# Route stage of a two-layer decoder trunk: choosing experts from PSUM operands, three tiles at once, and a fixed order into the first expert

## The chip, the cores and the metric

The kernel runs on one core of a Trainium2 chip. The metric is the device time of one execution in microseconds (us), from first to last instruction with what lies around them. Engines are named as the profile names them: PE (TensorE matmuls), PEld (TensorE weight loads), DVE (VectorE), ACT (ScalarE), POOL (GpSimd) and SP (SyncE, which issues most loads).

## The reference

The kernel computes a decoder trunk of two layers on 512 tokens of 1024 columns, in fp32. Layer 0 mixes by sliding-window attention and forgetting attention, layer 1 by sparse top-k attention and latent attention. Each mixer ends in an output projection; then come a layer norm, a mixture of 16 experts (hidden width 512) and a second layer norm:

```
for l in range(2):
    x = layer_norm(ALPHA * x + mixer[l](x), ln_g[l, 0], ln_b[l, 0])
    s = sigmoid(x @ router_w)                 # (512, 16)
    sel = s + router_b                        # 4 groups of 4 experts
    group = argmax over groups of (sum of the best two sel in the group)
    e1, e2 = the two experts of that group with the largest sel
    gate_j = s[e_j] / (s[e_1] + s[e_2])
    y = sum_j gate_j * (silu(x @ w_gate[e_j]) * (x @ w_up[e_j])) @ w_down[e_j]
    x = layer_norm(ALPHA * x + y, ln_g[l, 1], ln_b[l, 1])
```

The router's weights and bias are shared by both layers.

## The kernel before

The 512 tokens are four tiles of 128 rows, `xr[0]` to `xr[3]`. Every large product is made of three passes: a weight chunk of 1 MB is loaded into `wraw`, ScalarE rounds it to a high part (`wh`, L185, 128x1024 at a time), VectorE takes the low part (`wl`, L186), and `mm3` (L198 to L200) adds three matmuls. Activations are split alike by `split_to` (L203 on ScalarE, L204 on VectorE).

The route stage of a layer is `out_proj`. Its pieces run in the order that ROUTE_ORDER (L55) spells out: `y` i adds the second half of the output projection to tile i, in two column halves c (`half_proj`, twelve matmuls each; the sum and its statistics are L571 and L572 on VectorE), transposes the half (L576, TensorE), copies it to `yT` (L578, ScalarE) and multiplies it with the folded router weights into the logits `lgs` (L580, TensorE). `l` i makes mean and inverse deviation, the router's input `u` (L586, L587), the sigmoid `aff` (L588) and the layer norm (L589 on ScalarE, then multiplication by the gain and addition of the bias on GpSimd, L255 and L256; of tile 3 the last 256 columns on VectorE, by LN1_DVE). The normed tile goes to DRAM twice (`x1d`, `yd`, issued on POOL's queue, L591 and L594). `r` i j stands for `choose` (L413 to L454: group and two experts of tiles i to j - 1), `slots` (the place of each token among the tokens of expert 0, L477, and the mask `oh0`, L479) and `first_rows` (L490: the rows of the first expert collected by matmuls with the mask).

All of `choose` works on tiny tiles on VectorE, with operands in SBUF; `lgs` takes 128 of the 512 columns of its PSUM bank.

Then `moe` runs the experts. Each takes at most 96 tokens (CAP). Expert 0's rows come from `first_rows`, split by `put_rows` into `gH` and `gL`; those of the others are gathered from `x1d` by an indirect DMA with `idx`, which `after_slots` makes. `up` makes the gate product (24 mm3 matmuls in two chunks), then the up product; `hidden` transposes, `scatter` does the down product and adds the rows to `yd`. The weights of expert e are loaded by SP in the order in which buffers come free; the first sixteen loads are asked for in the order AHEAD, and `slot_of` gives each its buffer.

A planner puts the instructions of an engine in order by readiness; `tc.issue_after` adds an edge of order between two instructions of one engine, and `keep_in_program_order` fixes the order in which they were written. The order of operations on different engines follows from data and buffers.

Of the kernel before, what the change touches and what calls it, by code (L numbers as in the profile page):

```python
# [41 lines left out]
AHEAD = (2, 3, 4, 0, 1, 5, 6, 8, 9, 10, 12, 13, 7, 14, 11, 15)  # L42


LN1_DVE = (0, 0, 0, 256)
# [9 lines left out]
ROUTE_ORDER = "y0 l0 y1 l1 y2 l2 y3 l3 r02 r23 r34"  # L55
# [12 lines left out]
def trunk_kernel(ctx: ExitStack, tc, x_in, even_w_in, even_b_f, even_sinks, odd_w_in,  # L68
# [92 lines left out]
    hold = [None]  # L161
    in_order = [False]
# [25 lines left out]

    def ksplit(w, n, eng=V):

        rows = []
        for u in range(w.shape[1] // n):
            h, l = unit(w[:, u * n:(u + 1) * n, :], eng[u] if isinstance(eng, list) else eng)
            rows += [(h[:, j, :], l[:, j, :]) for j in range(n)]
        return rows

    def mm3(o, lh, ll, rh, rl, first, last):
        T.matmul(o, lh, rh, start=first, stop=False)  # L198
        T.matmul(o, lh, rl, start=False, stop=False)  # L199
        T.matmul(o, ll, rh, start=False, stop=last)  # L200

    def split_to(hdst, ldst, src):
        first(A.copy(hdst, src))  # L203
        first(V.tensor_tensor(out=ldst, in0=src, in1=hdst.bitcast(F32), op=ALU.subtract))  # L204

    def rsqrt(var, eps, n, pin=lambda ins: ins):
# [20 lines left out]
        c = square(q, v)  # L227
        pin(V.scalar_tensor_tensor(out=p, in0=c, scalar=-10.0 / 3, in1=c, op0=ALU.add, op1=ALU.mult))
# [184 lines left out]
    def choose(t0, t1):  # L413

        n = t1 - t0
        ts_ = slice(t0, t1)
        sel = sm.tile([128, NT, NE], F32, name="sel", bufs=1)[:, 0:n]
        V.tensor_tensor(out=sel, in0=aff[:, ts_], in1=rb.unsqueeze(1).to_broadcast([128, n, NE]), op=ALU.add)
        sg = sel.rearrange("p t (g j) -> p (t g) j", j=4)
# [12 lines left out]
        if n == 1:  # L432
            V.scalar_tensor_tensor(out=gs, in0=gs, scalar=gm, in1=desc4.unsqueeze(1), op0=ALU.is_equal, op1=ALU.mult)
            V.tensor_reduce(out=gm2, in_=gs, axis=AX.X, op=ALU.max)
            V.scalar_tensor_tensor(out=sg, in0=gs.rearrange("p t g -> p (t g)").unsqueeze(2).to_broadcast([128, 4, 4]),
                                   scalar=gm2, in1=sg, op0=ALU.subtract, op1=ALU.add)
        else:
            V.tensor_tensor(out=gs, in0=gs, in1=gm.unsqueeze(2).to_broadcast([128, n, 4]), op=ALU.is_equal)
            V.tensor_tensor(out=gs, in0=gs, in1=desc4.unsqueeze(1).to_broadcast([128, n, 4]), op=ALU.mult)
            V.tensor_reduce(out=gm2, in_=gs, axis=AX.X, op=ALU.max)  # L440
            V.tensor_tensor(out=gs, in0=gs, in1=gm2.unsqueeze(2).to_broadcast([128, n, 4]), op=ALU.subtract)
            V.tensor_tensor(out=sg, in0=gs.rearrange("p t g -> p (t g)").unsqueeze(2).to_broadcast([128, 4 * n, 4]),
                            in1=sg, op=ALU.add)
# [6 lines left out]
        f8 = sm.tile([128, NT, 2], F32, name="rf8")[:, 0:n]  # L450
# [3 lines left out]
        V.tensor_tensor(out=M[:, ts_], in0=O[:, ts_, 0, :], in1=O[:, ts_, 1, :], op=ALU.add)  # L454
# [12 lines left out]
    def slots(sl, oh0, t0, t1):  # L467
# [5 lines left out]
        for j in range(1, t1):  # L473
# [19 lines left out]
    def after_slots(sl, oht, flag):  # L493
# [913 lines left out]
```

## Time and profile before

| | |
|---|---|
| median of 3 runs | 1180.2 us (1179.53 to 1184.04) |
| the profiled execution | 1180.26 us |
| its span (first to last instruction) | 1178.5 us |
| mean granted TensorE clock | 0.954 |
| PE, DVE, ACT, POOL busy | 93%, 79%, 65%, 23% of the span |

A time of the trace counts from the start of the span. The shares are means over stages with different limits: attention in the first 240 us and from 540 to 820 us or so, the route stage of layer 0 around 225 to 272 us and of layer 1 around 810 to 860 us, and the experts behind each. A granted clock of 1 stands for 2.4 GHz; the lower of the two levels is 1.2 GHz.

### The profile page before, as it was taken

How to read it: one execution, taken by the hardware profiler on the slowest of the kernel's cores; microseconds unless marked ns; L12 is line 12 of the kernel's file. 1: busy time of each engine (PE TensorE's matmuls, PEld its weight loads, DVE VectorE, ACT ScalarE, POOL GpSimd, SP SyncE). 2: the span in 40 equal slices, each digit the busy share in tenths (PEclk: the TensorE clock that was granted, in tenths of full speed). 3: DMA queues.
4: the chain of work that ended last, by engine and by line, in shares of the span. 5: the costliest groups of instructions: out<-in, count | busy, mean ns of one | idle time of the engine just before them, and what ended most of it. 6: DMA issues, size and time to landing. Idle time of an engine off the chain costs nothing. (4 is left out here: it accounts for less than half of the span.)

```text
span 1178.5 us, 16701 instructions
## 1 busy us (share of the span) xinstructions
PE 1093.0 (93%) x5775; PEld 817.5 (69%) x5775; DVE 934.3 (79%) x1866; ACT 762.3 (65%) x1229; POOL 266.5 (23%) x223
## 2 busy tenths in 40 slices
PE   8999989979999999998599898999799999999982
PEld 7786767867777777776377665777677777777761
DVE  4646756597999999987766998766879999999976
ACT  4556646235888888887435744654268888888862
POOL 2001340251111141112613133003411111411023
PEclk9999999988999999999699998999789999999997
DMA  8314332779999997998512211335699999989972
GB/s 209 117 40 90 75 88 105 255 276 303 302 358 357 350 334 237 361 357 279 183 28 72 73 37 37 107 108 209 240 299 285 365 342 353 339 255 366 371 234 108
DMA packets 139613, 262.25 MB, mean 223 GB/s; under 512 B 11831, under 2 KB 28247, under 8 KB 139520
## 3 DMA queue, kind: packets, MB, share of 16 engines
q1 hardware_dynamic: 129232, 234.62, 57.9%
q0 software_dynamic: 10288, 26.48, 9.1%
q8 instruction: 47, 0.77, 0.3%
q14 instruction: 46, 0.38, 0.1%
HBM read 246.73 MB, written 22.30 MB: 228 GB/s over the span
## 5 line engine op out<-in xcount | busy, mean ns | idle before, releaser
L186 DVE TENSOR_TENSOR wl<-wraw,wh 128x1024 fp32r<-128x1024 f32 (+1 forms) x418 | 503.6, 1231 | 83.3 <-ACT wh L185 74.9
L185 ACT CAST wh<-wraw 128x1024 fp32r<-128x1024 f32 (+3 forms) x436 | 445.7, 1039 | 155.0 <-PE ps_s L200 63.8
L198 PE MATMUL ps_s<-wh,m 128*96 128x512 f32 (+1 forms) x528 | 208.3, 394 | 1.7 <-ACT m L203 1.7
L199 PE MATMUL ps_s<-wl,m 128*96 128x512 f32 (+1 forms) x528 | 206.4, 391 | 0.0
L200 PE MATMUL ps_s<-wh,m 128*96 128x512 f32 (+1 forms) x528 | 205.0, 388 | 0.4 <-DVE m L204 0.4
L200 PEld LDWEIGHTS ps_s<-wh,m 128*96 128x96 f32 x528 | 86.4, 164 | 35.7 <-DVE m L204 1.3
L198 PEld LDWEIGHTS ps_s<-wh,m 128*96 128x96 f32 x528 | 86.7, 164 | 34.8 <-ACT m L203 2.1
L199 PEld LDWEIGHTS ps_s<-wl,m 128*96 128x96 f32 x528 | 86.4, 164 | 31.9 <-issue 0.2
L198 PE MATMUL ps_a<-wh,hH 128*96 128x512 f32 x256 | 102.7, 401 | 3.8 <-ACT hH L203 3.8
L199 PE MATMUL ps_a<-wl,hH 128*96 128x512 f32 x256 | 101.8, 398 | 4.0 <-POOL wl L186 4.0
L200 PE MATMUL ps_a<-wh,hL 128*96 128x512 f32 x256 | 101.0, 394 | 1.3 <-DVE hL L204 1.3
L198 PE MATMUL ps_a<-wh,XH 128*128 128x512 f32 (+2 forms) x224 | 89.4, 399 | 4.3 <-ACT wh L185 3.2
L1100 POOL DMA_INDIRECT m<-x1d,idx x30 | 33.1, 1104 | 255.8 <-PE ps_t L1111 224.2
L200 PE MATMUL ps_a<-wh,XL 128*128 128x512 f32 (+2 forms) x224 | 88.7, 396 | 1.9 <-DVE XL L204 1.9
L1175 POOL DMA_INDIRECT yd<-m,idx x30 | 49.2, 1640 | 177.0 <-ACT m L1174 173.3
L199 PE MATMUL ps_a<-wl,XH 128*128 128x512 f32 (+2 forms) x224 | 88.8, 396 | 0.0
L199 PE MATMUL ps_a<-XL,wh 128*128 128x512 f32 x160 | 65.0, 406 | 0.0
L200 PE MATMUL ps_a<-XH,wl 128*128 128x512 f32 x160 | 64.7, 405 | 0.3 <-DVE wl L186 0.3
L198 PE MATMUL ps_a<-XH,wh 128*128 128x512 f32 x160 | 64.6, 403 | 0.0
L357 ACT ACTIVATE p<-p,nm 128x256 f32<-128x256 f32 (+3 forms) x96 | 50.6, 529 | 17.8 <-DVE nm L350 8.8
L376 ACT COPY pT<-ps_t 128x512 f32<-128x512 f32 (+2 forms) x88 | 43.4, 517 | 28.8 <-PE ps_t L373 28.0
L199 PEld LDWEIGHTS ps_a<-wl,hH 128*96 128x96 f32 x256 | 41.3, 161 | 20.5 <-POOL wl L186 5.4
(327 smaller groups left out, 1918.3 us busy)
## 6 DMA issues: line engine op xcount, KB each, us to landing
wraw<-in_moe_w_up_dram SPq DMA_DIRECT2D x64, 1024.0 KB
wraw<-in_moe_w_gate_dram SPq DMA_DIRECT2D x64, 1024.0 KB
wraw<-in_moe_w_down_dram SPq DMA_DIRECT2D x64, 1024.0 KB
wraw<-in_w_o_dram SPq DMA_DIRECT2D x6, 1024.0 KB
wraw<-in_even_w_in_dram SPq DMA_DIRECT2D x4, 1024.0 KB
x1d<-xr POOLq DMA_DIRECT2D x8, 512.0 KB
yd<-xr POOLq DMA_DIRECT2D x8, 512.0 KB
xr<-yd SPq DMA_DIRECT2D x8, 512.0 KB
```

Of the source, the lines that this page charges most:

```text
L185: first(A.copy(hv, w))
L186: first(eng.tensor_tensor(out=lv, in0=w, in1=hv.bitcast(F32), op=ALU.subtract))
L198: T.matmul(o, lh, rh, start=first, stop=False)
L199: T.matmul(o, lh, rl, start=False, stop=False)
L200: T.matmul(o, ll, rh, start=False, stop=last)
L357: A.activation(out=pt[h], in_=(pt if bias else Sp)[h], func=AF.Exp, bias=nm[:, h:h + 1], scale=(slopes[0][h] if slopes else 1.0), accum_ou ...
L376: A.copy(d_, s_)
L1100: G.indirect_dma_start(out=xg_of[e], out_offset=None, in_=x1d[:, :], in_offset=bass.IndirectOffsetOnAxis(ap=idx[:CAP, e:e + 1], axis=0), b ...
L1175: G.indirect_dma_start(out=yd[:, :], out_offset=bass.IndirectOffsetOnAxis(ap=idx[:CAP, e:e + 1], axis=0), in_=yos[e % 2], in_offset=None, ...
```

## The change

- ROUTE_ORDER becomes `y0 l0 y1 l1 y2 l2 c03 y3 s03 l3 r03`: `choose` runs once for tiles 0 to 2 and once for tile 3, and `slots` and `first_rows` of tiles 0 to 2 are pieces of their own.
- `choose` takes at most one operand from SBUF in each operation; the other lies in PSUM, in scratch columns of the bank that holds `lgs`. The sigmoid is written twice (PSUM and SBUF), the first sum too. The mask `M` becomes a reduction, `oh0` is made tile by tile, and the inverse deviation of one tile uses operations with one tensor operand.
- The statistics of tiles 0 and 1 come from accumulating instructions (`tensor_tensor_reduce` on VectorE, a square on ScalarE). Tile 3's layer norm is made on VectorE by halves (`centre`, `whole`); GpSimd's affine remains for tiles 0 to 2.
- `half_proj` of a tile's second column half holds its last nine matmuls behind the first half's logits (`behind`).
- Everything behind tile 3's `u` has a written order on VectorE: centre 0, choose, centre 1, slots, whole 0, low part 0, whole 1, put 0, low part 1, put 1, low part 2, then inside the first gate product `slot_tokens` and low part 3. The first expert's high parts come on ScalarE behind the sigmoid.
- `after_slots` is split in three: `slot_tokens` (the index, now in fp32), `slot_weights` (behind expert 0's up product) and `for_the_end` (transposed masks and overflow count, at expert 4).
- AHEAD moves load 7 (the second chunk of expert 0's up weights) to the end, and its buffer and that of two work tiles are exchanged. `hH` and `hL` become one tile. The router's folding is queued behind layer 0's last sum of the first half projection.

The core of the diff:

```diff
-AHEAD = (2, 3, 4, 0, 1, 5, 6, 8, 9, 10, 12, 13, 7, 14, 11, 15)
-LN1_DVE = (0, 0, 0, 256)
+AHEAD = (2, 3, 4, 0, 1, 5, 6, 8, 9, 10, 12, 13, 14, 11, 15, 7)
-ROUTE_ORDER = "y0 l0 y1 l1 y2 l2 y3 l3 r02 r23 r34"
+ROUTE_ORDER = "y0 l0 y1 l1 y2 l2 c03 y3 s03 l3 r03"
...
+    def high(w):
+        h, l = (hl.tile([128, 1024], F32R, name="w" + t.lower(), tag=t).rearrange("p (a b) -> p a b", a=2) for t in "HL")
+        return h, l, A.copy(h, w)
+    def low(w, h, l):
+        return V.tensor_tensor(out=l, in0=w, in1=h.bitcast(F32), op=ALU.subtract)
...
+    def scratch(p):
+        return (p[:, 0:64].rearrange("p (t e) -> p t e", e=NE), p[:, 64:128].rearrange("p (t e) -> p t e", e=NE),
+                p[:, 128:144].rearrange("p (t g) -> p t g", g=4), p[:, 144:152].rearrange("p (t c) -> p t c", c=2))
...
-    def choose(t0, t1):
+    def choose(t0, t1, sc):
+        affp, selp, gp, f8 = (t[:, ts_] for t in sc)
-        V.tensor_tensor(out=sel, in0=aff[:, ts_], in1=rb.unsqueeze(1).to_broadcast([128, n, NE]), op=ALU.add)
+        for t in (selp, sel):
+            V.tensor_tensor(out=t, in0=affp, in1=rb.unsqueeze(1).to_broadcast([128, n, NE]), op=ALU.add)
-        V.tensor_tensor(out=pr[:, :, 0:2], in0=sg[:, :, 0:2], in1=sg[:, :, 2:4], op=ALU.add)
+        V.tensor_tensor(out=pr[:, :, 0:2], in0=sg[:, :, 0:2], in1=sp[:, :, 2:4], op=ALU.add)
...
-        V.tensor_tensor(out=M[:, ts_], in0=O[:, ts_, 0, :], in1=O[:, ts_, 1, :], op=ALU.add)
+            return V.tensor_reduce(out=M[:, ts_], in_=O[:, ts_].rearrange("p t c e -> p t e c"), axis=AX.X, op=ALU.add)
...
-        return V.tensor_tensor(out=oh0[:, t0:t1], in0=slot1.unsqueeze(1).to_broadcast([128, n, CAP]),
-                               in1=sl[:, t0:t1, 0:1].to_broadcast([128, n, CAP]), op=ALU.is_equal)
+        for i in range(t0, t1):
+            oh = V.tensor_scalar(oh0[:, i, :], slot1, sl[:, i, 0:1], None, op0=ALU.is_equal)
...
+    def slot_tokens(sl, room):
+        for h in range(2):
+            oh = room()[:, 0:4 * CAP].rearrange("p (j s) -> p j s", j=4)
+            V.tensor_tensor(out=oh, in0=slot1.unsqueeze(1).to_broadcast([128, 4, CAP]),
+                            in1=pos[:, 4 * h:4 * h + 4].unsqueeze(2).to_broadcast([128, 4, CAP]), op=ALU.is_equal)
...
-    def half_proj(chunk, oH, oL, g, i):
+    def half_proj(chunk, oH, oL, g, i, behind=None):
+            with tc.issue_after(behind.ins) if behind and k else nullcontext():
+                mm3(o, oH[4 * g + k][:, ts_], oL[4 * g + k][:, ts_], *chunk[k], k == 0, k == 3)
...
-            lgs = ps_s()[:, 0:2 * NT * NE].rearrange("p (c t e) -> p c t e", c=2, t=NT)
+            bank = ps_s()
+            lgs = bank[:, 0:2 * NT * NE].rearrange("p (c t e) -> p c t e", c=2, t=NT)
+            sc = scratch(bank[:, 2 * NT * NE:512])
...
+                if by_act(i):
+                    V.tensor_tensor_reduce(out=ys, in0=o, in1=ys, scale=1.0, scalar=(ls[:, i, 0:1] if c else 0.0),
+                                           op0=ALU.add, op1=ALU.add, accum_out=ls[:, i, c:c + 1])
...
+                A.activation(out=sc[0][:, i, :], in_=u[:, i, :], func=AF.Sigmoid)
+                end["act"] = A.activation(out=aff[:, i, :], in_=u[:, i, :], func=AF.Sigmoid)
...
+        def centre(h):
+            return V.scalar_tensor_tensor(out=ys, in0=ys, scalar=end["mu"], in1=gb[:, cs], op0=ALU.subtract, op1=ALU.mult)
+        def whole(h):
+            return V.scalar_tensor_tensor(out=ys, in0=ys, scalar=end["rs"], in1=bb[:, cs], op0=ALU.mult, op1=ALU.add)
...
+        with tc.issue_after(end["u"].ins):
+            c0 = centre(0)
+        with tc.issue_after(c0.ins):
+            chosen = choose(n, NT, sc)
+        with tc.issue_after(chosen.ins):
+            c1 = centre(1)
+        with tc.issue_after(c1.ins):
+            oh = slots(sl, oh0, n, NT)
...
-                t = xo.tile([128, 2048], F32, name="wraw3", tag=dict(e=eH, E=eL, l=lL, x=lH)[t])
+                t = xo.tile([128, 2048], F32, name="wraw3", tag=dict(e=eH, E=eL, l=eL, x=lH)[t])
...
+        in_turn(lambda: route["whole"](0))
+        route["rows"](0)
+        low_part(0)
+        in_turn(lambda: route["whole"](1))
+        route["rows"](1)
+        route["x1"]()
+        in_turn(lambda: put_rows(0, ps2[0]))
+        low_part(1)
+        in_turn(lambda: put_rows(1, ps2[1]))
+        low_part(2)
+        def between():
+            with tc.issue_after(last_mm[0].ins):
+                in_turn(lambda: found.extend(slot_tokens(sl, route["room"])) or found[0])
+            low_part(3)
+            for i in (1, 2):
+                gather(i)
...
+            if e == 4:
+                with tc.issue_after(act_op[0].ins):
+                    for_the_end(sl, oht, flag)
```

## Rows read from the trace of the kernel before

**Rows 1.** The page's first part: busy time, share of the span, instructions of each engine.

```profile
PE 1093.0 (93%) x5775; PEld 817.5 (69%) x5775; DVE 934.3 (79%) x1866; ACT 762.3 (65%) x1229; POOL 266.5 (23%) x223
```

**Rows 2.** Windows: length, busy time (instructions) PE, PEld, DVE, ACT, POOL; clock, DMA share, GB/s.

```profile
240.00:250.00 10.00, 7.42 (x25) 6.27 (x26) 8.10 (x35) 3.82 (x5) 3.00 (x3) 0.66 0.59 231
...
300.00:440.00 140.00, 140.00 (x667) 99.54 (x666) 130.27 (x128) 119.61 (x144) 30.35 (x20) 1.00 1.02 343
...
830.00:840.00 10.00, 10.00 (x44) 8.07 (x44) 5.60 (x12) 5.47 (x7) 3.83 (x2) 0.65 0.08 18
```

**Rows 3.** Timeline of PE, both layers: start, duration, operation, count, [idle before <-releaser].

```profile
236.47 1.03 PE L580 MATMUL ps_s<-rwgb,yT 128*128 128x16 f32 x8
...
238.13 0.39 PE L200 MATMUL ps_a<-wh,XL 128*128 128x512 f32 x1
238.36 0.39 PE L198 MATMUL ps_a<-wh,XH 128*128 128x512 f32 x1
...
242.58 0.66 PE L576 MATMUL ps_t<-ident,xr 128*128 128x128 f32 x4 [2.90 <-DVE xr L571]
...
247.27 0.63 PE L200 MATMUL ps_a<-wh,XL 128*128 128x512 f32 x1
247.70 0.63 PE L198 MATMUL ps_a<-wh,XH 128*128 128x512 f32 x1
...
279.52 0.40 PE L200 MATMUL ps_s<-wh,m 128*96 128x512 f32 x1
...
287.65 0.47 PE L198 MATMUL ps_s<-wh,m 128*96 128x512 f32 x1 [0.85 <-ACT m L203]
...
823.24 0.40 PE L200 MATMUL ps_a<-wh,XL 128*128 128x512 f32 x1
...
874.85 0.48 PE L198 MATMUL ps_s<-wh,m 128*96 128x512 f32 x1 [0.85 <-ACT m L203]
```

**Rows 4.** Timeline of DVE and POOL in layer 0's route stage.

```profile
229.19 2.37 POOL L256 TENSOR_TENSOR xr<-xr,lnt 128x1024 f32<-128x1024 f32 x1
229.21 0.69 DVE L571 TENSOR_TENSOR xr<-xr,ps_a 128x512 f32<-128x512 f32 x1 [1.79 <-PE ps_a L200]
...
237.41 2.46 POOL L256 TENSOR_TENSOR xr<-xr,lnt 128x1024 f32<-128x1024 f32 x1
...
237.51 2.40 DVE L423 TENSOR_TENSOR pr<-sel 128x16 f32<-128x16 f32 x1
...
241.85 0.67 DVE L571 TENSOR_TENSOR xr<-xr,ps_a 128x512 f32<-128x512 f32 x1
```

**Rows 5.** Timeline of layer 1's tail, DVE, PE and ACT.

```profile
845.40 0.23 DVE L587 SCALAR_TENSOR_TENSOR u<-ps_s,rs_o,u 128x16 f32<-128x16 f32 x1
...
850.88 0.16 DVE L418 TENSOR_TENSOR sel<-aff,rb 128x16 f32<-128x16 f32 x1
...
853.51 0.17 DVE L454 TENSOR_TENSOR M<-O 128x16 f16<-128x16 f16 x1
...
855.15 0.17 DVE L477 SCALAR_TENSOR_TENSOR sl<-ps_s,M 128x16 f32<-128x16 f32 x1 [1.27 <-PE ps_t L517]
...
855.76 1.99 PE L490 MATMUL ps_o<-oh,xr 128*128 128x96 f32 x8 [0.62 <-DVE oh L479]
...
857.83 0.48 ACT L203 CAST m<-ps_o 128x384 fp32r<-128x384 f32 x1 [11.04 <-issue]
```

**Rows 6.** Groups by line: operation, count | busy, mean ns | idle before it, releasers.

```profile
L186 DVE TENSOR_TENSOR wl<-wraw,wh 128x1024 fp32r<-128x1024 f32 (+1 forms) x418 | 503.6, 1231 | 83.3 <-ACT wh L185 74.9
...
L204 DVE TENSOR_TENSOR m<-ps_t,m 128x384 fp32r<-128x384 f32 x60 | 30.6, 551 | 0.0
...
L578 ACT COPY yT<-ps_t 128x512 f32<-128x512 f32 x16 | 9.3, 586 | 33.3 <-PE ps_t L576 33.3
```

**Rows 7.** Timeline of layer 0's mixer: two engines reading one PSUM tile.

```profile
82.30 0.42 ACT L709 COPY vt<-ps_a 128x316 f32<-128x316 f32 x1 [3.13 <-PE ps_a L200]
...
82.76 0.17 DVE L710 TENSOR_TENSOR z<-ps_a,bf 128x8 f32<-128x8 f32 x1 [3.38 <-ACT vt L709]
```

More of the change, by code (lines that the diff above doesn't have):

```diff
@@ L161, in trunk_kernel @@
     hold = [None]
+    late = [None]
     in_order = [False]
@@ L199, in mm3 @@
         T.matmul(o, lh, rl, start=False, stop=False)
-        T.matmul(o, ll, rh, start=False, stop=last)
+        last_mm[0] = T.matmul(o, ll, rh, start=False, stop=last)
     def split_to(hdst, ldst, src):
         first(A.copy(hdst, src))
-        first(V.tensor_tensor(out=ldst, in0=src, in1=hdst.bitcast(F32), op=ALU.subtract))
+        return first(V.tensor_tensor(out=ldst, in0=src, in1=hdst.bitcast(F32), op=ALU.subtract))
     def rsqrt(var, eps, n, pin=lambda ins: ins):
@@ L566, in out_proj, with room, by_act @@
         rows = [ksplit(wload(chunk_src(c, g), 4, 512), 2) for c in range(2)]
+        def room():
+            return work.tile([128, 512], F32, name="yT", tag="sg", bufs=2)
+        def by_act(i):
+            return main and i < 2
+        sts = [sm.tile([128, 2, 6], F32, name="st", tag="st", bufs=4) for _ in range(NT)]
         def tile_y(i):
@@ new lines, in tile_ln @@
+                A.activation(out=sc[0][:, i, :], in_=u[:, i, :], func=AF.Sigmoid)
+                end["act"] = A.activation(out=aff[:, i, :], in_=u[:, i, :], func=AF.Sigmoid)
+            if i == NT - 1 or not main:
+                end.update(mu=mv[:, 0, 0:1], rs=rs)
+                return
+            nm = sm.tile([128, 1], F32, name="nmr", bufs=4)
+            if by_act(i):
+                V.tensor_scalar(nm, ls[:, i, 2:3], 32.0, rs, op0=ALU.mult, op1=ALU.mult)
+            else:
+                V.tensor_scalar(nm, mv[:, 0, 0:1], -1.0, rs, op0=ALU.mult, op1=ALU.mult)
@@ L591, in tile_ln, with x1 @@
+            with tc.issue_after(end["act"].ins):
+                A.activation(out=xr[i], in_=xr[i], func=AF.Identity, scale=rs, bias=nm)
+            affine(xr[i], gb, bb, 0)
+            x1(i)
+        def x1(i):
             nc.gpsimd.dma_start(x1d[i * 128:(i + 1) * 128, :], xr[i])
@@ L607, in out_proj, with last_rows @@
                 tile_ln(i)
-            else:
-                j = int(n[1])
-                if i == 0:
-                    ps2 = [ps_o(), ps_s()]
-                choose(i, j)
-                slots(sl, oh0, i, j)
-                first_rows(ps2, oh0, i, j)
-        return sl, ps2, oht
+            elif f == "c":
+                choose(i, int(n[1]), sc)
+            elif f == "s":
+                slots(sl, oh0, i, int(n[1]))
+            else:
+                for c, k in enumerate(("y", "lg")):
+                    with tc.issue_after(end[k].ins):
+                        first_rows(ps2, oh0, i, int(n[1]), (c,))
+        n = NT - 1
+        with tc.issue_after(end["u"].ins):
[6 more added lines that the diff above has]
+            oh = slots(sl, oh0, n, NT)
+        def last_rows(h):
+            first_rows(ps2, oh0, n, NT, (h,))
+        return sl, ps2, oht, dict(oh=oh, act=end["act"], whole=whole, rows=last_rows, x1=lambda: x1(n), room=room)
     def even_mixer():
@@ L1204, in moe @@
             sg = act(g, u, n)
+            if e == 0:
+                with tc.issue_after(put.ins):
+                    slot_weights(found[1])
             if e < last:
@@ L1297, in dense_moe @@
             A.activation(out=aff, in_=lgs, func=AF.Sigmoid)
-            choose(0, NT)
+            sc = scratch(ps_o())
+            V.tensor_copy(sc[0], aff)
+            choose(0, NT, sc)
             weights()
```

166 lines of the change are left out of this document (98 added, 68 removed).

## Prediction

> **What bounds the kernel now.** I read the page's busy shares first: TensorE is busy 93% of the span [rows 1], so only a stretch in which it idles or runs slowly can give much back. The windows say where that is. In the expert loop TensorE is busy 140.00 of 140 us at clock 1.00, with the DMA share at 1.02 [rows 2]: nothing on VectorE or ScalarE is to be won there. The windows on the route stage show the opposite: the granted clock is 0.66 in 240 to 250 us and 0.65 in 830 to 840 us, a mix of the two levels, 2.4 and 1.2 GHz [rows 2].
>
> TensorE's timeline gives the reason. The second half projection of tile 2 (call its end E) ends at 238.5 us in layer 0 and 823.6 in layer 1. Soon after, TensorE stands 2.90 us, released by VectorE's residual sum of that half. Behind the stall, matmuls follow each other every 0.43 us (247.27 to 247.70), before it every 0.23 [rows 3]. So a stall of about 3 us was followed by some 7 us at the lower level; the same place of layer 1 has the 0.65 [rows 2].
>
> Who makes VectorE late? The sum at 241.85 is queued behind `choose` of tiles 0 and 1, and of that one addition of 16 numbers a row takes 2.40 us (237.51), exactly while GpSimd runs its 2.4 us multiplications of layer norm (237.41). The sum of 229.21 has one operand in PSUM and ran beside a GpSimd instruction of the same kind in its usual 0.69 us [rows 4]. Two SBUF operands wait for GpSimd; one does not.
>
> The tail repeats it. In layer 1 tile 3's `u` is ready at 845.63, but VectorE then does its quarter of the layer norm beside GpSimd, so `choose` of tile 3 starts only at 850.88 and ends at 853.68 (2.80 us); the slots follow at 855.15, the row products run at half pace (1.99 us for eight), and the second expert's first matmul comes at 874.85 [rows 3, 5].
>
> **The change, part by part.** I count from E to expert 1's first matmul; behind that, TensorE sets the pace. Before, that is 287.65 - 238.52 = 49.1 us in layer 0 and 874.85 - 823.64 = 51.2 in layer 1 [rows 3].
>
> *One SBUF operand each.* The contended additions fall to some 0.2 us. Some 14 operations of the three-tile `choose` and 11 of the one-tile one now touch PSUM. Does that cost more? `sl`, which reads PSUM, takes 0.17 us; an addition in SBUF beside nothing took 0.16 [rows 5]. Lower bound 0; upper bound 0.07 each (`u` reads PSUM in 0.23) [rows 5], 25 x 2 x 0.07 = 3.5 us. I take 0.
>
> *Tile 3 without turns between engines.* Without the stall TensorE runs tile 3's first half at once: 12 x 0.23 = 2.8. The sum 0.69, transposes some 0.7, copy 0.59, logits 1.03 [rows 3, 4, 6] bring it to E+6.0. The nine matmuls held behind these logits end at E+8.2 and cost about 0.3 us against running them early, as TensorE has nothing else. Sum, transposes, copy, logits again 3.0, hand-overs of about 0.1 each, `u` 0.46: E+12.75. Sigmoid some 0.35; VectorE centres the first half beside it (0.69). `choose` measured 2.80 and grows by a doubled first sum and a reduction for the mask, 3.2 in all: E+16.7. Then second centring 0.7 (E+17.4), slots 0.45, one half of the affine 0.69 (E+18.55). The eight row products at full pace take 0.9, the copy 0.48 [rows 5], hand-overs 0.7: first expert matmul E+20.7.
>
> *The fixed order on VectorE.* The first expert's four low parts, 1.23 each [rows 6], were done during tile 3 before; now they are queued in the tail. From E+18.55: low 1.23, whole 0.69, put 0.55, low 1.23, put 0.55, low 1.23, `slot_tokens` 3.2, low 1.23 [rows 6]. (The 3.2 is an estimate: two masks of 384 columns at 0.55, as the low part of that size [rows 6]; three operations on 128 columns, between the 0.16 of 32 and that 0.55, at 0.3 [rows 5]; the matmuls and the index 1.2.) That is 28.6; six last matmuls 1.4 and hand-overs: gate ends at E+30.5. VectorE, not TensorE, sets this. In layer 0 the second expert follows the end of the first gate by 7.7 us (279.92 to 287.65) [rows 3]; with 0.3 for the moved load, 8.0 gives E+38.5. Gains 10.6 and 12.7: 23.3 us.
>
> *Turns on one PSUM bank.* The new scratch columns lie in the bank of the router's logits. Three-tile `choose` (25 operations at about 0.19, from about E+4.3, since it needs tile 2's sigmoid) works in it until E+9, and tile 3's first logits write into the same bank at E+5.1. The trace has one case of two engines at different columns of one bank: VectorE's `z` (columns 316 to 324) starts at 82.76, only after ScalarE's copy of columns 0 to 316 (82.30, 0.42 long), with 3.38 us idle put down to it [rows 7]. I take it that the logits wait as `z` did: they start at E+9.0, 3.9 late, and by the `behind` edge nine projection matmuls wait too. At full clock, less the 0.9 us that VectorE would have made the second half late anyway, 3.0 us a layer. But 3.9 us is longer than the 2.90 that was followed by the lower level. At 0.43 instead of 0.23, nine matmuls cost 1.8 more, and logits, transposes and the second logits another 1.4: 6.2 a layer. Gains 4.4 and 6.5, 10.9 together.
>
> The Trainium skill, "PSUM — Partial Sum Buffer", section "PSUM bank collisions raise a hardware error", speaks against this change: it says that two engines on one bank and partition quadrant must not meet even at different columns, and that the compiler's scheduler therefore adds a dependency between them. The trace agrees in its one case (`z` at 82.76). By it the stall is certain; without it the sum would be the 23.3 above.
>
> *Smaller parts.* Tiles 0 and 1 take the variance on ScalarE (a square of 1024 columns, about 1.2) instead of two VectorE statistics of 0.69; both lie under TensorE's projections: 0, at most 0.5 a layer if it delays a copy to `yT`. Second sigmoid write 0.2, in the sum. GpSimd loses its tile-3 affine; `x1d` and `yd` of tile 3 are issued after the second `whole`, far ahead of the gathers: 0. The count of overflowing tokens and the transposed masks move to expert 4, some 0.3 of TensorE a layer either way: 0. Loads: u1c1 is asked for last and waits for the first gate; it is needed 5 us later, so it may cost 0 to 1. The queue is kept full through the loop [rows 2]: if loads did not come earlier with the issues, a gain would be eaten later; but issues on SP follow buffers that TensorE frees, so I take 0. Sum of small gains 1.
>
> Sum against the profiled execution, 1180.26 us (span 1178.5, 1.8 around it; the median 1180.2 is 0.06 away): 1180.3 - 10.9 - 1 = **1168**.
>
> **The rivals.**
> (a) The logits wait, but the clock stays at 2.4 GHz: 3.0 a layer, 1180.3 - 17.3 = 1163. For it: TensorE has run at 1.00 without a break up to E, and one stall is thin; against it, both layers show the lower level at this place [rows 2].
> (b) No waiting for the bank: 1180.3 - 23.3 = 1157. For it: one example is thin, and the order of the two could be exchanged, logits first. Against: the example.
> (c) Loads eat it: the DMA share is 1.02 in the loop; if half of 12 comes back as waits of ScalarE on loads, 1174.
> (d) No change: `choose` at 25 operations, handed over to and from TensorE, or queued behind VectorE's other work, ends 5.5 us later than I have it, which both layers pay: 1168 + 11 = 1179.
> (e) Slower: an operand in PSUM is dear for a chain of short dependent operations. With 50 on the path, +0.22 us each eats the 11; from +0.34 each the kernel is over 0.5% slower (1186). `sl`'s 0.17 speaks against it [rows 5], but that one has no PSUM operation right ahead of it, as these have.
>
> **How the numbers follow.** Chances: forecast 0.44, (a) 0.18, (b) 0.16, (c) 0.06, (d) 0.08, (e) 0.08. 0.5% is 5.9 us, about what a measurement here can tell from no change. Faster are the first four, less a little of (c): 0.82; same 0.10; slower 0.08. Low end: (b) less 3 for small gains, 1154. High end: the forecast with 3.5 for PSUM and 5 from (c), 1177. (d), (e) and a tail below 1154 are left out, 0.2 together.
>
> **What would show it.** Right: no VectorE addition above 0.3 us beside GpSimd in `choose`; TensorE idle 3 to 4 us near E+5 to E+9, released by an operation of the three-tile `choose`; matmuls every 0.43 us behind it; `choose` of tile 3 right after `u`; the first expert at about E+27, the second at E+45. Wrong for (b) if there is no such wait; for (a) if 0.23 goes on; for (c) if ScalarE waits on loads in the loop; for (e) if the PSUM operations are 0.3 us or their pitch 0.4. The forecast fails most if `choose` is moved on VectorE against tile 3's sums, or if `slot_tokens` takes far from 3.2 us.

## The result and the profile after

The changed kernel takes 1196.6 us (median of four runs, 1193.91 to 1201.05) against 1182.02 for the kernel before in the same comparison: a ratio of 1.0128, 95% interval 1.0085 to 1.0171. The forecast was 1168; the kernel is slower, and by a mechanism that none of the rivals names. The profiled execution took 1193.91 us (span 1192.1), 13.65 more than the one before. One of the nine runs of e5 below, at a granted clock of 0.644 (1586.87 us), is left out of its ratio.

The page's busy line, which answers to [rows 1], differs little:

```profile
PE 1094.6 (92%) x5787; PEld 815.0 (68%) x5787; DVE 922.4 (77%) x1818; ACT 765.9 (64%) x1243; POOL 262.6 (22%) x219
```

The windows [rows 2] do. The columns are those of before: length, busy time of PE, PEld, DVE, ACT, POOL, granted clock, DMA share, GB/s.

```profile
250.00:260.00 10.00, 7.47 (x28) 5.69 (x29) 4.01 (x22) 0.43 (x1) 5.30 (x4) 0.55 0.42 147
...
280.00:300.00 20.00, 17.20 (x71) 12.48 (x71) 13.20 (x19) 10.48 (x13) 5.57 (x3) 0.76 1.01 336
310.00:450.00 140.00, 140.00 (x672) 99.64 (x671) 129.75 (x130) 119.16 (x143) 29.74 (x19) 1.00 1.01 343
```

Ten us of the route stage have a clock of 0.55, and 280 to 300 us, in which the first two experts run, 0.76. In the loop TensorE is busy throughout, as before.

VectorE and GpSimd in layer 0's route stage and first expert (answers to [rows 4] and [rows 5]; start, duration, engine, line):

```profile
249.49 2.33 POOL L272 TENSOR_TENSOR xr<-xr,lnt 128x1024 f32<-128x1024 f32 x1 [1.80 <-ACT xr L662]
...
250.37 0.20 DVE L467 TENSOR_TENSOR sel<-gs,ps_s 128x48 f32<-128x48 f32 x1
...
251.61 0.26 DVE L476 TENSOR_TENSOR O<-io,ps_s 128x96 f16<-128x96 f32 x1
...
257.93 0.69 DVE L624 TENSOR_TENSOR xr<-xr,ps_a 128x512 f32<-128x512 f32 x1 [5.78 <-PE ps_a L210]
...
262.92 0.17 DVE L443 TENSOR_TENSOR ps_s<-ps_s,rb 128x16 f32<-128x16 f32 x1
...
265.67 0.19 DVE L479 TENSOR_REDUCE M<-O 128x16 f16<-128x32 f16 x1
...
277.98 0.17 DVE L537 TENSOR_SCALAR idx<-ps_s 96x16 uint32<-96x16 f32 x1 [1.73 <-PE ps_s L535]
...
279.03 4.61 POOL L1204 DMA_INDIRECT m<-x1d,idx  x1 [8.23 <-DVE idx L537]
279.20 4.85 DVE L186 TENSOR_TENSOR wl<-wraw,wh 128x1024 fp32r<-128x1024 f32 x4
...
283.97 0.30 DVE L484 TENSOR_TENSOR gt<-O,aff 128x128 f32<-128x128 f16 x1
...
287.10 0.16 DVE L488 TENSOR_TENSOR as__2920<-a 128x4 f32<-128x4 f32 x1
287.35 1.23 DVE L186 TENSOR_TENSOR wl<-wraw,wh 128x1024 fp32r<-128x1024 f32 x1
288.49 0.17 DVE L489 RECIPROCAL as__2920<-as__2920 128x4 f32<-128x4 f32 x1
...
290.08 0.29 DVE L542 TENSOR_TENSOR og<-O,gates 128x128 f32<-128x128 f16 x1
```

`choose` does what the change says: 0.15 to 0.3 us an operation even beside GpSimd's multiplication (249.49), 2.94 us for tile 3 (262.92 to 265.86). Further down, the index comes 8.6 us behind the first expert's first matmul (269.40), the gather takes GpSimd 4.61 us beside four low parts in a row, and the small steps from `gt` to `og` wait behind low parts of 1.23 us.

TensorE, same stretch, and two rows of layer 1 (answers to [rows 3]):

```profile
245.95 1.06 PE L633 MATMUL ps_s<-rwgb,yT 128*128 128x16 f32 x8 [0.29 <-ACT yT L631]
...
252.01 1.86 PE L633 MATMUL ps_s<-rwgb,yT 128*128 128x16 f32 x8 [4.99 <-DVE O L476]
...
254.70 0.63 PE L210 MATMUL ps_a<-wh,XL 128*128 128x512 f32 x1
255.13 0.63 PE L208 MATMUL ps_a<-wh,XH 128*128 128x512 f32 x1
...
269.40 0.74 PE L208 MATMUL ps_s<-wh,m 128*96 128x512 f32 x1 [0.57 <-ACT m L213]
...
279.34 0.62 PE L209 MATMUL ps_s<-wl,m 128*96 128x512 f32 x1 [1.39 <-DVE wl L195]
...
290.43 2.74 PE L546 MATMUL ps_t<-og,yT 128*96 128x16 f32 x16 [2.80 <-DVE og L542]
293.00 1.52 PE L1215 MATMUL ps_t<-ident,m 96*128 96x96 f32 x8
294.45 0.74 PE L208 MATMUL ps_s<-wh,m 128*96 128x512 f32 x1
...
848.01 1.86 PE L633 MATMUL ps_s<-rwgb,yT 128*128 128x16 f32 x8 [4.99 <-DVE O L476]
...
887.08 1.52 PE L1215 MATMUL ps_t<-ident,m 96*128 96x96 f32 x8
```

The logits of tile 3's first half stand 4.99 us in both layers until VectorE's last scratch operation of the three-tile `choose` (L476), the pitch behind (from one matmul's start to the next) is 0.43 us (254.70 to 255.13), and the rows of expert 1 are transposed (L1215) only at 293.00 and 887.08. Before, that was 285.97 (L1111).

To compare kernels I cut the profiled executions at marks that all have. A is VectorE's last sum of the first half projection (215.38 us in layer 0 before, 217.28 after). The other marks are the last residual sum, the first expert's first matmul, and the transposes of expert 1's and of expert 2's rows. Each cell is layer 0 / layer 1, in us, differences of starts in the timelines of one execution, so its sums need not follow the medians to the microsecond. The labels are those of the experiments below.

| kernel | A to last sum | to first matmul | to expert 1's rows | to expert 2's rows |
|---|---|---|---|---|
| before | 36.8 / 59.5 | 20.4 / 21.0 | 13.4 / 13.5 | 13.7 / 13.6 |
| after | 40.7 / 64.0 | 11.5 / 11.4 | 23.6 / 22.1 | 14.0 / 13.9 |
| e5_index_early | 40.7 / 64.3 | 12.5 / 15.7 | 19.7 / 19.5 | 15.3 / 14.8 |
| e6_own_bank2 | 36.6 / 58.2 | 14.6 / 15.6 | 23.7 / 20.7 | 14.1 / 14.1 |
| e8_both_no_behind | 31.6 / 53.0 | 16.5 / 15.6 | 18.4 / 19.0 | 14.6 / 14.2 |
| e9_chain_whole | 31.5 / 52.8 | 18.1 / 16.5 | 14.7 / 15.4 | 13.1 / 12.8 |
| b1_operands_only | 35.1 / 56.4 | 17.5 / 16.7 | 15.1 / 14.2 | 15.8 / 13.1 |
| e12_no_behind_alone | 30.8 / 51.7 | 17.6 / 17.9 | 23.7 / 22.1 | 14.2 / 13.9 |

From A to the first matmul the change gains 5.1 and 5.2 us. In the next column it loses 10.2 and 8.6. That, and not the route stage, is where it became slower than before.

### The profile page after: what moved, and what is told of

It reads as the page before. It is cut to its first block, busy times and chain, and to the rows that moved or that the text cites. A ratio compares the mean times of both kernels' runs of the same rounds, so it can differ in the third digit from the quotient of the medians.

```text
span 1192.1 us, 16678 instructions
## 1 busy us (share of the span) xinstructions
PE 1094.6 (92%) x5787; PEld 815.0 (68%) x5787; DVE 922.4 (77%) x1818; ACT 765.9 (64%) x1243; POOL 262.6 (22%) x219
## 4 chain that ended last, share of the span: by engine, by line
PE 37%; DVE 9%; ACT 2%; POOL 1%; issue 1%; DVEq 0%; POOLq 0%; ACTq 0%
PE ps_s L208 5%; PE ps_s L210 5%; PE ps_s L209 5%; PE ps_a L208 5%; PE ps_a L210 5%; PE ps_a L209 5%; DVE sc L1080 1%; PE ps_o L397 1%; PE ps_t L390 1%; DVE m L1079 1%; PE ps_s L1105 1%; PE ps_t L1215 1%; DVE nm L369 1%; DVE mx L364 1%; PE ps_s L633 1%
## 5 line engine op out<-in xcount | busy, mean ns | idle before, releaser
L186 DVE TENSOR_TENSOR wl<-wraw,wh 128x1024 fp32r<-128x1024 f32 (+1 forms) x410 | 494.6, 1233 | 83.5 <-ACT wh L185 74.8
L185 ACT CAST wh<-wraw 128x1024 fp32r<-128x1024 f32 (+3 forms) x428 | 437.3, 1038 | 154.9 <-PE ps_s L210 71.9
L209 PE MATMUL ps_s<-wl,m 128*96 128x512 f32 (+1 forms) x528 | 206.6, 391 | 2.8 <-DVE wl L195 2.8
L209 PEld LDWEIGHTS ps_s<-wl,m 128*96 128x96 f32 x528 | 87.2, 165 | 37.1 <-DVE wl L195 3.2
L209 PE MATMUL ps_a<-wl,h 128*96 128x512 f32 x256 | 101.3, 396 | 5.8 <-POOL wl L186 5.8
L208 PE MATMUL ps_a<-wh,h 128*96 128x512 f32 x256 | 102.8, 402 | 3.7 <-ACT h L213 3.7
L210 PE MATMUL ps_a<-wh,h 128*96 128x512 f32 x256 | 101.7, 397 | 1.3 <-DVE h L214 1.3
L1204 POOL DMA_INDIRECT m<-x1d,idx x30 | 37.4, 1247 | 253.9 <-PE ps_t L1215 236.9
L209 PE MATMUL ps_a<-wl,XH 128*128 128x512 f32 (+2 forms) x224 | 87.1, 389 | 0.0
L209 PE MATMUL ps_a<-XL,wh 128*128 128x512 f32 x160 | 64.6, 404 | 0.0
L209 PEld LDWEIGHTS ps_a<-wl,h 128*96 128x96 f32 x256 | 41.6, 163 | 22.9 <-POOL wl L186 7.1
```

The costliest lines, as they stand in the source:

```text
L185: first(A.copy(hv, w))
L186: first(eng.tensor_tensor(out=lv, in0=w, in1=hv.bitcast(F32), op=ALU.subtract))
L210: last_mm[0] = T.matmul(o, ll, rh, start=False, stop=last)
L1204: G.indirect_dma_start(out=xg_of[e], out_offset=None, in_=x1d[:, :], in_offset=bass.IndirectOffsetOnAxis(ap=idx[:CAP, e:e + 1], axis=0), b ...
```

## The experiments

Each ratio is against the kernel before on the same chip, whose median there was 1178.97 to 1180.86 us (1182.02 beside the changed kernel). Where two kernels were measured beside different runs of the kernel before, their ratios are compared and not their medians. The first four runs took the visible waits: the shared bank, and what delays expert 1.

**e1_own_bank.** The scratch of `choose` goes to free columns of the bank that collects the first rows.

```diff
-            sc = scratch(bank[:, 2 * NT * NE:512])
+            ps2 = [ps_o(), ps_s()]
+            sc = scratch(ps2[0][:, 4 * CAP:512])
```

> The changed kernel, but the scratch of choose lies in the free columns of the bank that collects the first expert's rows, not in the bank of the logits. Theory (turns on one bank): tile 3's logits no longer stand 4.99 us behind the three-tile choose, the matmuls behind them keep 0.23 us instead of 0.43; the last residual sum comes 5 to 6 us earlier in each layer (252 instead of 257.93 in layer 0), the first expert's first matmul too, and the time falls by 9 to 12 us to about 1186. Rival (the chain of short VectorE operations on PSUM operands sets the tail, whichever bank they are in): the stall goes, the first expert's first matmul moves by under 2 us, time 1193 or more.

1198.84 us, ratio 1.0158 (1.0134 to 1.0181). The wait on L476 is gone, but it turned up elsewhere. On VectorE:

```profile
267.05 0.18 DVE L443 TENSOR_TENSOR ps_o<-ps_o,rb 128x16 f32<-128x16 f32 x1 [6.57 <-PE ps_o L516]
```

`choose` of tile 3 now waits 6.57 us for the row products, which write other columns of that bank. So in these two kernels a bank went from engine to engine as a whole, in the written order, and the next try gave the scratch a bank that almost nobody else writes.

**e2_weights_later.** The gate weights (`slot_weights`, the chain from `gt` to `og`) move from behind expert 0's up product into expert 1's gate product.

```diff
-            if e == 0:
-                with tc.issue_after(put.ins):
-                    slot_weights(found[1])
+        def weigh():
+            with tc.issue_after(last_mm[0].ins):
+                slot_weights(found[1])
...
+            g = up("g", e, *((None, 1, weigh if e == 1 else None) if e else (g0, 1, between)))
```

> The changed kernel, but slot_weights stands on TensorE's queue inside expert 1's gate product instead of ahead of expert 1's transposes. Theory (TensorE's queue): the 2.80 us wait for og, its 2.74 us of matmuls and the half pace of the transposes (1.52 instead of 0.82) go from the path; expert 1's transposes start at 288 instead of 293.0 in layer 0 and at 882 instead of 887.1 in layer 1, time 9 to 11 us lower, about 1187. Rival (expert 1's rows are late anyway, since the index comes at 278 and the first gather takes 4.61 us on GpSimd's queue): the transposes wait for the gathered rows, under 1.5 us a layer is won, time 1194 or more.

1196.99 us, 1.0171 (1.0128 to 1.0214): nothing won. TensorE's waits from 240 to 305 us (engine, tile and line that waited, what it waited for, us, times, longest) show why:

```profile
PE ps_s L633 <- DVE O L476: 5.0, 1, 5.0
PE ps_t L1215 <- DMA m<-x1d,idx: 3.5, 1, 3.5
```

Without the wait on `og`, the gather itself is late. The transposes started at 288.15, 7.45 us after GpSimd's instruction of 276.09 to 280.70 had ended. Expert 2's rows came 16.7 us behind expert 1's instead of 14.0: the matmuls on `og` (1.45 us) now stand between them; the rest of the difference is not explained.

**e3_low_first.** Low part 3 goes ahead of `slot_tokens`.

```diff
         def between():
+            low_part(3)
             with tc.issue_after(last_mm[0].ins):
                 in_turn(lambda: found.extend(slot_tokens(sl, route["room"])) or found[0])
-            low_part(3)
```

> The changed kernel, but VectorE makes the first gate's last low part before slot_tokens instead of behind it. Theory (the gate stands behind slot_tokens): TensorE's wait of 1.4 us for that low part and the lower clock behind it go; expert 0's products end 3 to 4 us earlier in each layer, but slot_weights still stands ahead of expert 1, so expert 1 starts only 1 to 3 us a layer earlier: time 1191 to 1195. Rival (the index, 1.2 us later, holds expert 1): expert 1's transposes do not move or come later, 1197.

1189.2 us, 1.0083 (1.0025 to 1.0140), below the 1191 to 1195 that I expected, but with an interval that overlaps the changed kernel's. The wait of L209 on `wl` went and one of 1.5 us on the masks of `slot_tokens` came. The gather took 1.41 us here, not 4.61.

**e4_all_three** puts the three edits together.

> All three edits together. Theory (three places where TensorE's queue stands, each followed by a lower clock): expert 1's transposes come 11 to 13 us earlier than in the changed kernel in each layer (about 281 and, 11 more, 863 to 865), time about 1172, below the kernel before. Rival (the three hide behind one another, VectorE's fixed order sets the end): 1182 or more.

1197.9 us, 1.0157 (1.0118 to 1.0195): a miss. The transposes wait 4.7 us for the gather. The edits open the same wait from several sides, and the row collector's bank (e1) costs more than it saves: its first matmul comes 3.6 and 1.9 us later, counted from A. The gather starts 0.9 us behind the index, so the next runs brought that forward.

**e5_index_early.** `slot_tokens` moves ahead of low part 0, the index behind `put_rows` 0; `slot_weights` goes into expert 0's up product.

```diff
-        low_part(0)
         in_turn(lambda: route["whole"](1))
-        route["rows"](1)
         route["x1"]()
+        in_turn(tokens)
+        route["rows"](1)
+        low_part(0)
         in_turn(lambda: put_rows(0, ps2[0]))
+        in_turn(lambda: slot_index(found[0]))
+        for i in (1, 2):
+            gather(i)
         low_part(1)
         in_turn(lambda: put_rows(1, ps2[1]))
         low_part(2)
+        low_part(3)
```

> The changed kernel with another order behind slots on VectorE: whole 0, whole 1, slot_tokens, low part 0, put 0, the index, then low part 1, put 1, low parts 2 and 3; slot_weights stands inside expert 0's up product. Theory (expert 1 waits for its rows: index, then a gather of 1 to 5 us on GpSimd, then some 7.4 us until the rows are there): the index comes about 15 us behind the last residual sum instead of 20, expert 1's transposes come 7 to 9 us earlier in each layer, counted from the last residual sum (35.1 us behind it in layer 0 of the changed kernel, then 26 to 28), and the time falls by 14 to 18 us to about 1180. Rival (the low parts, now later, hold the gate product, so VectorE sets expert 1 whatever the index does): expert 1's transposes within 2 us of where they were, time 1193 or more.

1190.01 us, 1.0087 (1.0062 to 1.0111). The index is written at 270.98, 7.0 us earlier, and the stretch from the first matmul to expert 1's rows falls from 23.6 and 22.1 to 19.7 and 19.5. But `slot_tokens` now stands ahead of the first matmul, which comes 1.1 and 4.5 us later from A; up to expert 1's rows the profiled execution is 2.8 us better in layer 0 and 2.0 worse in layer 1. Two waits remain, and the gather is as long as in the changed kernel:

```profile
PE ps_t L551 <- DVE og L547: 3.0, 1, 3.0
PE ps_t L1221 <- DMA m<-x1d,idx: 2.2, 1, 2.2
```

```profile
267.97 0.53 POOL L673 DMA_DIRECT2D x1d<-xr  x1 [12.94 <-DVE pt L525]
...
276.86 4.98 POOL L1210 DMA_INDIRECT m<-x1d,idx  x1 [7.84 <-ACT wh L185]
```

The gather starts 5.7 us behind the index, and what held it is the write of tile 3's normed rows to `x1d`, which it reads: issued at 267.97, it landed 7.9 us later, at 275.9, and the gather started 0.96 us behind that. In nine places of the runs (both layers of e5, e7 and e8, layer 1 of the changed kernel, e6 and e12) the gather starts 0.95 to 1.04 us behind this landing; in layer 0 of the changed kernel, e6 and e12, where the index comes later than the landing, it starts 0.88 us behind the index. So bringing the index forward uncovered the next thing that the gather needs.

**e6_own_bank2.** The scratch, and the place products of `slots`, get a third bank of their own.

```diff
-            sc = scratch(bank[:, 2 * NT * NE:512])
+            own = ps_s()
+            sc = scratch(own)
...
-        pp = ps_s()
...
-            oh = slots(sl, oh0, n, NT)
+            oh = slots(sl, oh0, n, NT, own[:, 256:320])
```

> The changed kernel with choose's scratch in a PSUM bank of its own (shared only with the counts pp of slots, whose matmuls come between the two chooses). Theory (turns): tile 3's logits wait only for tile 2's u (about 1.4 us) instead of 4.99 us for the three-tile choose, and choose of tile 3 follows its sigmoid at once; the last residual sum comes 3 to 5 us earlier against the eighth sum of the first half, and so does everything behind it: 1187 to 1190. Rival (as in the first try, the wait moves to the tail): last residual sum to first expert matmul grows from 11.5 to over 15 us, time 1196 or more.

1188.92 us, 1.0083 (1.0051 to 1.0115), within the range that I expected, 0.45% (some 5 us) under the changed kernel. The intervals of e5 and of e6 each overlap the changed kernel's; only both together (e7) stand clear of it. The wait of 4.99 us is gone; the logits wait 1.4 us for `u`, which still reads their bank. From A the last sum comes 4.1 and 5.7 us earlier, but the first matmul only 1.0 and 1.5.

**e7_both** is e5 and e6 together, **e8_both_no_behind** is that without the `behind` edge:

```diff
-                o = half_proj(rows[c], oH, oL, g, i, end.get("lg") if main and c else None)
+                o = half_proj(rows[c], oH, oL, g, i, None)
```

> Early index and own bank together. Theory (two separate causes, a stall ahead of the tail and a late index behind it): the gains add, 1168 to 1175, below the kernel before. Rival (they overlap): not below 1180.

> The same without the edge that holds the last nine projection matmuls behind the first half's logits. Theory (a stall of TensorE costs twice, as wait and as lower clock behind it): the nine matmuls fill the remaining wait for tile 2's u, no stall and no matmuls at 0.43 us before the tail, another 2 to 3 us a layer, 1164 to 1170. Rival (the edge keeps the order that the tail needs; without it the first half's logits and the statistics come later): within 1 us of the run before, or slower.

e7 takes 1182.5 us (1.0035, 1.0004 to 1.0066), 0.93% under the changed kernel, against 0.41 and 0.45 for e5 and e6: the two repairs add up, but the time is the rival's (not below 1180), as e5 had won less than I expected. e8 takes 1176.55 us (0.9968, 0.9939 to 0.9997): the edge that I had put at 0.3 us a layer costs 6 here. It still fell short of the 1164 to 1170 that I expected, and its waits name the rest:

```profile
PE ps_t L550 <- DVE og L546: 3.0, 1, 3.0
PE ps_t L1221 <- DMA m<-x1d,idx: 1.4, 1, 1.4
```

**e9_chain_whole** is e8 with the chain from `gt` to `og` written as one piece right behind low part 3, and the low parts of the up weights behind it. **e10_chain_mid** puts it between low part 1 and `put_rows` 1.

```diff
         low_part(3)
+        in_turn(lambda: slot_weights(found[1]))
...
-            u = up("u", e, None, n, None if e else weigh)
+            with nullcontext() if e else tc.issue_after(put.ins):
+                u = up("u", e, None, n, None if e else weigh)
```

> The last kernel (early index, own bank, no edge behind the logits), and the small operations that lead to og now follow one another on VectorE right behind low part 3, with the up weights' low parts behind them. Theory (TensorE's stall for og, 3.0 us and the lower clock behind it, comes from low parts of 1.23 us that stand between the six small operations): the stall goes or is under 0.5 us, expert 1's transposes come 3 to 5 us earlier, time 1167 to 1171. Rival (the up weights' low parts, pushed back by the chain, stop TensorE instead, or the gathered rows do): less than 1.5 us a layer, 1174 to 1177.

> As the run before, but the small operations stand between low part 1 and put 1, so that GpSimd's first gather can run beside them and not beside back-to-back low parts. Theory (the gather takes 4.6 to 5.9 us instead of 1.1 because VectorE runs low parts back to back): the first gather ends within 2.5 us, the gathered rows no longer hold expert 1, time 1164 to 1169. Rival (the gather's length has another cause): it stays over 4 us, and low parts 2 and 3, 1.5 us later, hold the gate: 1172 or more.

e9 takes 1163.75 us, 0.9849 (0.9802 to 0.9896): faster than both kernels, and more than I expected. e10 takes 1168.51 us, 0.9896 (0.9848 to 0.9943); why it is behind e9, though its marks are not, is not explained. In e9's timeline the chain is whole, and the gather short:

```profile
273.66 0.28 DVE L484 TENSOR_TENSOR gt<-O,aff 128x128 f32<-128x128 f16 x1
...
274.50 0.18 DVE L489 RECIPROCAL as__2850<-as__2850 128x4 f32<-128x4 f32 x1
274.71 0.17 DVE L490 TENSOR_TENSOR gates<-a,as__2850 128x8 f32<-128x8 f32 x1
274.91 0.29 DVE L546 TENSOR_TENSOR og<-O,gates 128x128 f32<-128x128 f16 x1
274.99 1.17 POOL L1216 DMA_INDIRECT m<-x1d,idx  x1 [7.22 <-DVE gates L490]
...
283.18 0.82 PE L1227 MATMUL ps_t<-ident,m 96*128 96x96 f32 x8
```

The six steps take 1.54 us (273.66 to 275.20), against 6.4 in the changed kernel (283.97 to 290.37). What the whole chain and what the shorter gather (1.17 us, in e8 5.64) is worth, e9 does not separate. TensorE's largest waits from 240 to 300 us are now 1.2 and 0.9:

```profile
PE ps_o L515 <- DVE xr L692: 1.2, 1, 1.2
PE ps_s L209 <- DVE wl L186: 0.9, 1, 0.9
```

and in the second of these windows the clock is back (the columns as above):

```profile
240.00:260.00 20.00, 17.97 (x99) 15.35 (x98) 14.64 (x77) 8.20 (x15) 12.75 (x10) 0.81 0.94 345
260.00:300.00 40.00, 37.34 (x211) 28.14 (x211) 33.07 (x46) 23.45 (x30) 6.00 (x6) 0.97 0.85 289
```

In the same two windows the granted clock is 0.74 and 0.83 in the changed kernel, 0.83 and 0.87 in the kernel before.

e10 came within its range, but not for its reason. Its gathers are short, yet not beside the small operations, which had ended 3.3 us earlier; they ran inside a row of low parts:

```profile
273.26 8.06 DVE L186 TENSOR_TENSOR wl<-wraw,wh 128x1024 fp32r<-128x1024 f32 x7
273.91 1.52 POOL L1216 DMA_INDIRECT m<-x1d,idx  x1 [8.01 <-DVE wl L195]
275.73 1.85 POOL L1216 DMA_INDIRECT m<-x1d,idx  x1 [0.31 <-issue]
```

**b1_operands_only** goes from the other side: the kernel before, with PSUM operands in `choose` (scratch in a bank of its own) and `choose` of tiles 0 and 1 written ahead of tile 2, as its planner had run it. The smaller edits of `choose`, `slots` and the inverse deviation that go with the operands (the mask as a reduction, `oh0` tile by tile, the second sigmoid) are in it, nothing else of the change.

```diff
-ROUTE_ORDER = "y0 l0 y1 l1 y2 l2 y3 l3 r02 r23 r34"
+ROUTE_ORDER = "y0 l0 y1 l1 r02 y2 l2 r23 y3 l3 r34"
...
-        V.tensor_tensor(out=pr[:, :, 0:2], in0=sg[:, :, 0:2], in1=sg[:, :, 2:4], op=ALU.add)
+        V.tensor_tensor(out=pr[:, :, 0:2], in0=sg[:, :, 0:2], in1=sp[:, :, 2:4], op=ALU.add)
```

> The kernel before with one part of the change alone: choose, slots and the inverse deviation with one SBUF operand each, scratch in a PSUM bank of its own, choose of tiles 0 and 1 written ahead of tile 2 so that it need not wait for later sigmoids; after_slots, the loads, the low parts and the layer norm stay. Theory (the operands part does what it was forecast to do: no addition of 2.4 us, no stall of 2.9 us and no lower clock behind it): last residual sum 4 to 6 us earlier in each layer, choose as fast as before, time 1168 to 1173. Rival (operands in PSUM cost as much as they save, or handing the bank over does): 1178 or more.

1174.34 us, 0.994 (0.9918 to 0.9963). The groups of instructions from 230 to 262 us (busy us, mean ns of one, idle before) show the additions of `choose` cheap; their first ones, from 240.06 us on, ran beside GpSimd's multiplication (238.90 to 241.29):

```profile
L433 DVE TENSOR_TENSOR ps_s<-ps_s,rb 128x32 f32<-128x32 f32 (+1 forms) x2 | 0.4, 182 | 0.1
...
L437 DVE TENSOR_TENSOR pr<-sel,ps_s 128x16 f32<-128x16 f32 (+1 forms) x2 | 0.3, 160 | 0.0
```

The stall of 2.90 us is gone, but the last sum comes only 1.7 and 3.1 us earlier from A, not 4 to 6, and the time is a little above the 1168 to 1173 that I expected. So the part that the title names first, with a bank of its own, is worth 0.6%. The rest of the change, the shared bank among it, lost that again, and more.

**e12_no_behind_alone** is the changed kernel with the `behind` edge as its only edit, the same line as in e8.

> The changed kernel without the edge that holds nine of the last twelve projection matmuls behind the first half's logits; all else as changed. Theory (the wait for the bank costs most because those nine matmuls stand behind it): the nine matmuls run ahead of the waiting logits, the last residual sum comes 3 to 5 us earlier against the eighth sum of the first half (36 to 38 instead of 40.6 us in layer 0), and 1189 to 1193 is measured, since the late index keeps expert 1 where it is behind the tail. Rival (the edge costs 0.3 us a layer, as forecast, and the wait costs the same with or without it): within 1 us of the changed kernel's stage, 1196.

1183.17 us, 1.0036 (1.0009 to 1.0064), 0.92% (some 11 us) under the changed kernel and more than either side expected, with the shared bank, the late index and the broken chain all in place. TensorE's timeline, with the last scratch operation on VectorE:

```profile
250.37 0.66 PE L629 MATMUL ps_t<-ident,xr 128*128 128x128 f32 x4 [0.60 <-DVE xr L624]
...
252.73 0.24 DVE L476 TENSOR_TENSOR O<-io,ps_s 128x96 f16<-128x96 f32 x1
...
253.12 2.68 PE L633 MATMUL ps_s<-rwgb,yT 128*128 128x16 f32 x16 [2.09 <-DVE rs_r L241]
```

Both halves' logits of tile 3 (x16) run together behind one wait of 2.09 us. The profile puts it down to `rs_r`, which the logits do not read; L476 ends 0.15 us ahead of them, as in the changed kernel (0.14), so it is still the turn on the bank. The projections, the sum and the transposes had filled the rest of the time: the last sum comes 8.4 and 8.3 us behind this execution's E, where the prediction without any wait has E+8.2; in the changed kernel it comes 17.8 and 17.5 behind.

## Why the prediction was wrong

**Right.** The additions beside GpSimd fell to 0.2 us. PSUM operands are not dear: `choose` of tile 3 took 2.94 us against my 3.2, so rival (e) fell, although its side (slower) came true. The pitch behind the stall was 0.43. The logits took turns with the scratch in both layers, as the Trainium skill's "PSUM — Partial Sum Buffer" (section "PSUM bank collisions raise a hardware error") has it for different columns of one bank; 4.99 here and e1's 6.57 agree. From the last sum to the first matmul I had worked out about 12 us, and it took 11.5 and 11.4. Three slips change little: the terms up to E+12.75 give about 12.2, those up to 28.6 give 28.5, and GpSimd's instruction at 237.41 is the addition of the bias, not a multiplication.

**The step that failed: "the second expert follows the end of the first gate by 7.7 us ... with 0.3 for the moved load, 8.0 gives E+38.5."** I carried a distance over from a trace in which the work that sets it lay elsewhere. Before, the index was written at 275.29, 2.7 us behind the first matmul (272.57), the gather was issued at 275.75 and took GpSimd 1.08 us, and `og` was made at 276.03: all inside the first gate, and the rows were transposed 9.1 us after the gather's instruction had ended (276.83 to 285.97). The change moves the index to 8.6 us behind the first matmul and the gate weights behind the gate. I costed `slot_tokens` as VectorE time (3.2; it took 3.8) ahead of the gate's last low part, but not the gather that waits for it, and `slot_weights` not at all. From the end of that low part to expert 1's first matmul the forecast has 9.9 (28.6 to 38.5); it took 15.2 in both layers (279.28 to 294.45, 873.34 to 888.53). The write to `x1d` that I had put "far ahead of the gathers: 0" landed 1.1 us ahead of the index in layer 0 and 0.8 behind it in layer 1. From the first matmul to expert 1's rows the forecast has a loss of 5.3 us over both layers (17.8 each to expert 1's first matmul, against 15.1 and 15.2 before); measured is 18.8, so 13.5 us are missing. e2 and e4 show the gather as the next wait. e5 gets 6.5 of the stretch back with the early index, but gives 5.6 of it up ahead of the first matmul and then waits for `x1d`; e9 gets another 7.3 against e8, with the whole chain and a short gather. Removing only the one that ends last uncovers the next; for that reason e2 won nothing.

**A second step: `behind`, "about 0.3 us against running them early, as TensorE has nothing else."** TensorE had these nine matmuls to run during the wait, and the edge forbade it. I did count them behind the wait under "turns", 6.2 us a layer for both, but as the price of the bank. It is mostly that of the edge: without it 2.1 us of waiting for the bank are left and the last sum is not late (e12), and with it a bank of its own brings only 1.0 and 1.5 us to the first matmul (e6). A bank of its own without the edge was run only together with the early index (e8). The wait was also longer and later than forecast. The edge acts on every tile: in layer 1 TensorE waits 1.7 us for the statistics and 0.8 for a sum of earlier tiles, which neither the kernel before nor e12 shows, and the three-tile `choose`, which can't begin before tile 2's `u`, ends some 2.6 and 4.9 us behind my E+9, counted from A (in e12, without the edge, 2.2 and 1.6). From A to the first matmul I forecast gains of 7.2 and 9.1 us, and got 5.1 and 5.2: 6.0 missing. e12 gains 3.7 and 5.8 there over the changed kernel.

**A third, small: `for_the_end` at 0.** Experts 2 to 14 take 1.1 us longer in each layer (from 229.58 to 230.67 between expert 2's and expert 15's rows in layer 0). Some 0.7 of it is at expert 4, where the moved masks run; the remaining 0.03 us per expert, which b1 shows too, is not explained.

**The sum.** Forecast -12.3, profiled +13.65; of the 25.9 between them, 13.5 lie in the first expert, 6.0 ahead of it, 0.6 between experts 1 and 2, 2.2 in the later experts, 1.9 ahead of A (where the kernels' runs scatter from 214 to 219 us), 1 is the gain that I had allowed for small parts; 0.7 is left.

**The other rivals.** (a) fell with the pitch, (b) with the wait. (d) has this in it, that the three-tile `choose` ended late, but not for its 25 operations, which took 4.0 us: it began late, as tile 2's `u` did. (c) would need ScalarE to wait for loads; TensorE is busy for all of the 140 us of the loop, so it is not what happened. My early idea of one culprit fell with e1, e2 and e4. By the ratios, e12 gains some 11 us, e5 and e6 together (e7) 11 and e9 against e8 14. These overlap: each is what its edit is worth in its company, and they don't add to one account. e12's marked stretches, up to expert 2's rows, give 9.2.

## What to carry to other kernels

A distance read from a trace ("B follows A by 8") holds only while the work that hides under it stays there: for each piece moved, list what consumes it, a gather above all, and ask when that is due; for a gather ask too when the rows that it reads have landed. An edge of order is to be priced together with the longest wait that can come ahead of it, since it turns another's idle time into its own. A chain of short dependent steps should be written as one piece, because a planner that fills its gaps with 1.2 us instructions makes it four times as long.

## What the runs showed of the hardware

The first indirect gather of layer 0 took GpSimd 1.08 us before, 4.61 in the changed kernel, 5.94 in e1, 4.98 in e5, 1.41 in e3, 1.17 in e9 and 1.52 in e10. The long ones ran beside low parts in a row, which take two fp32 operands from SBUF. The Trainium skill's "SBUF — State Buffer" (section "SBUF: two separate sides") says that of a VectorE operation with two SBUF inputs and a GpSimd operation that reads SBUF, the one that starts first has the pair of ports that they share for its whole instruction, and the other waits. The long gathers agree with it, if a gather counts as such an operation for its index, which lies in SBUF. It does not tell the long gathers from the short ones: e10's, begun inside a row of low parts too, took 1.52 and 1.20 us (layers 0 and 1). What makes the gather long stays open.

Where TensorE waited for the gather (e2, e4, e5, e7 and e8, and layer 1 of e9 and b1), its transposes began 6.3 to 7.7 us after GpSimd's instruction had ended; the DMA share was 1.01 in 280 to 300 us of the changed kernel.
